# Instance normalisation bound by DMA: engine programs without a block, a first store that waits for half of the fourth load, and a last tile in three pieces

## The chip, the cores and the metric

One core of one Trainium2 chip. The metric is device time in microseconds (us) of one execution; lower is better. "Span" is the time from the first to the last instruction in a profiled execution. Every run quoted was classed fast unless it is said otherwise; each ratio is of kernels run in the same rounds on one chip. Where medians of different rounds, and so of different chips, are set side by side, the text says so; the kernel before had medians of 1248.44 to 1248.65 us in all of them.

## The reference

```python
x: (8, 64, 32, 64, 64) float32
mean = np.mean(x, axis=(2, 3, 4), keepdims=True)
var = np.var(x, axis=(2, 3, 4), keepdims=True)
return ((x - mean) / np.sqrt(var + eps)).astype(np.float32)
```

There are 512 instances of 131,072 elements, 268 MB in and 268 MB out, and each instance needs its own mean and variance.

## The kernel before

A tile holds 8 instances: 128 partitions of 8192 columns, 4 MB (16 partitions for an instance). Six slots in SBUF take turns. SyncE loads, VectorE and ScalarE each sum half of the columns, TensorE averages over the partitions of an instance with a small matrix, ScalarE squares, takes the root, and both engines scale half of the tile in place. ScalarE then issues the store. A load into a slot waits for the store of the tile that was there before. Of 64 tiles, 60 run in loops of six, three more are written out, and the last is cut in halves.

```python
    block = ctx.enter_context(nc.Block())

    @block.sync
    def _(eng):
        for s in range(SLOTS):
            eng.dma_start(out=slots[s][:], in_=x_t[s]).then_inc(landed[s], 16)
        ...
        with eng.Fori(1, ROUNDS) as it:
            for s in range(SLOTS):
                eng.dma_start(out=slots[s][:], in_=x_t[it * SLOTS + s])._wait_ge(
                    stored[s], c16
                ).then_inc(landed[s], 16)
    ...
    def on_scalar(eng, t, lane, n, c1, c2, c16, dst):
        # (cut: sum, squares with accumulation, square root)
        eng.activation(out=t[:, :w], in_=t[:, :w], func=Act.Identity,
            scale=a[:, 5:6], bias=a[:, 6:7],
        )._wait_ge(shifted[lane], c1).then_inc(done[lane], 1)
        eng.dma_start(out=dst, in_=t)._wait_ge(done[lane], c2).then_inc(stored[lane], 16)
```

## Time and profile before

| | before |
|---|---|
| time, median of 3 runs | 1248.36 us (1248.33 to 1248.52) |
| span of the profiled run | 1246.9 us |
| DMA | full in all slices but the first two and the last, 431 GB/s over the span |
| ScalarE busy | 986 us, 79% |

Read this kernel from its DMA: no compute engine limits it. The prediction below shows the slices and windows. From the page's DMA issues (KB of each, median us from issue to landing):

```profile
slot<-in_x_dram SPq DMA_DIRECT2D x63, 4096.0 KB, 52.8
out_dram<-slot ACTq DMA_DIRECT2D x63, 4096.0 KB, 45.3
```

A tile passes every 19.4 us, so 2.7 loads and 2.3 stores stand in their queues at any time; neither queue runs empty.

From its timeline, the issue of the first and of the last store on ScalarE (start, duration):

```profile
31.85 0.40 ACTq L130 DMA_DIRECT2D out_dram<-slot  x1
...
1233.92 0.34 ACTq L130 DMA_DIRECT2D out_dram<-slot  x1
```

And the last microseconds in the windows view, whose last two columns are DMA share and GB/s:

```profile
1242.00:1244.00 2.00, 0.00 (x0) 0.00 (x0) 0.00 (x0) 0.00 (x0) 0.00 (x0) 1.00 0.44 188
1244.00:1245.00 1.00, 0.00 (x0) 0.00 (x0) 0.00 (x0) 0.00 (x0) 0.00 (x0) 1.00 0.04 16
1245.00:1246.00 1.00, 0.00 (x0) 0.00 (x0) 0.00 (x0) 0.00 (x0) 0.00 (x0) 1.00 0.00 0
```

### The profile page before, as it was taken

How to read it: one execution, taken by the hardware profiler on the slowest of the kernel's cores; microseconds unless marked ns; L12 is line 12 of the kernel's file. 1: busy time of each engine (PE TensorE's matmuls, PEld its weight loads, DVE VectorE, ACT ScalarE, POOL GpSimd, SP SyncE). 2: the span in 40 equal slices, each digit the busy share in tenths (PEclk: the TensorE clock that was granted, in tenths of full speed). 3: DMA queues.
4: the chain of work that ended last, by engine and by line, in shares of the span. 5: the costliest groups of instructions: out<-in, count | busy, mean ns of one | idle time of the engine just before them, and what ended most of it. 6: DMA issues, size and time to landing. Idle time of an engine off the chain costs nothing.

```text
span 1246.9 us, 1819 instructions
## 1 busy us (share of the span) xinstructions
PE 76.4 (6%) x260; PEld 65.2 (5%) x260; DVE 467.9 (38%) x325; ACT 986.1 (79%) x410; POOL 1.9 (0%) x11
## 2 busy tenths in 40 slices
PE   0000000000000000000000000000000000000000
PEld 0000000000000000000000000000000000000000
DVE  2344334433334334343343433433334333343331
ACT  5888888887787878778777878787787878778774
POOL 0000000000000000000000000000000000000000
DMA  9999999999999999999999999999999999999998
GB/s 403 422 435 427 433 436 435 428 433 436 435 428 433 437 434 429 432 436 435 431 430 436 436 434 425 437 436 435 427 434 436 435 428 433 436 435 428 433 432 376
DMA packets 18723, 536.90 MB, mean 431 GB/s; under 512 B 2081, under 2 KB 2081, under 8 KB 2081
## 3 DMA queue, kind: packets, MB, share of 16 engines
q1 hardware_dynamic: 9360, 268.44, 50.0%
q10 hardware_dynamic: 9360, 268.44, 49.9%
q14 instruction: 3, 0.02, 0.0%
HBM read 268.44 MB, written 268.44 MB: 431 GB/s over the span
## 4 chain that ended last, share of the span: by engine, by line
ACT 48%; DVE 29%; another core or an unknown queue 13%; PE 6%; issue 1%; DMA 1%; ACTq 0%; DVEq 0%; SPq 0%
ACT unused L113 37%; DVE small L79 18%; DVE slot L95 8%; ACT slot L123 4%; ACT unused L107 4%; PE psum L136 3%; PE psum L143 3%; ACT small L120 1%; ACT L120 1%; DMA slot<-in_x_dram 1%; DVE small L89 1%; DVE small L82 1%; DVE small L92 1%; ACTq L130 0%
## 5 line engine op out<-in xcount | busy, mean ns | idle before, releaser
L113 ACT ACTIVATE unused<-slot,small 128x8192 uint8<-128x8192 f32 (+1 forms) x65 | 456.1, 7017 | 90.1 <-DVE small L82 90.1
L79 DVE TENSOR_REDUCE small<-slot 128x1 f32<-128x4096 f32 (+1 forms) x65 | 282.9, 4353 | 164.4 <-DMA slot<-in_x_dram 164.4
L107 ACT ACTIVATE unused<-slot 128x4096 uint8<-128x4096 f32 (+1 forms) x65 | 231.7, 3564 | 82.1 <-DMA slot<-in_x_dram 77.0
L123 ACT ACTIVATE slot<-slot,small 128x4096 f32<-128x4096 f32 (+1 forms) x65 | 243.7, 3749 | 27.6 <-DVE small L92 27.6
L89 DVE RECIPROCAL small<-small 128x1 f32<-128x1 f32 x65 | 10.6, 164 | 533.8 <-ACT small L120 533.8
L95 DVE TENSOR_SCALAR slot<-slot,small 128x4096 f32<-128x4096 f32 (+1 forms) x65 | 154.7, 2379 | 2.4
L136 PE MATMUL psum<-small,avg 128*128 128x2 f32 x130 | 38.2, 363 | 674.1 <-DVE small L79 548.7
L136 PEld LDWEIGHTS psum<-small,avg 128*128 128x128 f32 x130 | 32.6, 311 | 679.6 <-DVE small L79 553.0
L143 PE MATMUL psum<-small,avg 128*128 128x1 f32 x130 | 38.2, 363 | 480.6 <-ACT unused L113 480.6
L143 PEld LDWEIGHTS psum<-small,avg 128*128 128x128 f32 x130 | 32.7, 312 | 486.2 <-ACT unused L113 486.2
L120 ACT ACTIVATE small<-psum,eps_t 128x1 f32<-128x1 f32 x65 | 17.0, 261 | 37.4 <-PE psum L143 37.3
L82 DVE TENSOR_REDUCE small<-psum 128x1 f32<-128x2 f32 x65 | 10.3, 159 | 62.5 <-PE psum L136 62.5
L107 ACT ACT_TABLE_LOAD x10 | 12.8, 1283 | 10.4 <-ACT slot L123 7.1
L120 ACT ACT_TABLE_LOAD x10 | 12.8, 1283 | 0.2
L107 ACT ACTIVATION_READ_ACCUMULATOR unused<-slot 128x1 f32 x65 | 12.1, 186 | 0.0
L113 ACT ACTIVATION_READ_ACCUMULATOR unused<-slot,small 128x1 f32 x65 | 12.1, 186 | 0.0
L92 DVE TENSOR_TENSOR small<-small 128x1 f32<-128x1 f32 x65 | 10.3, 159 | 2.2
L208 POOL TENSOR_SCALAR_AFFINE_SELECT avg<-avg 128x128 f32<-128x128 f32 x4 | 1.3, 324 | 0.3
L205 POOL MEMSET avg<- 128x128 f32 x2 | 0.4, 204 | 0.5 <-SPq L42 0.5
L257 POOL MEMSET const-bfloat16-1.0<- 128x1 bf16 x1 | 0.1, 101 | 0.0
L257 POOL MEMSET const-uint8-127<- 128x1 uint8 x1 | 0.1, 101 | 0.0
L257 POOL MEMSET const-float32-0.0<- 128x1 f32 x1 | 0.1, 98 | 0.3 <-issue 0.3
(2 smaller groups left out, 0.2 us busy)
## 6 DMA issues: line engine op xcount, KB each, us to landing
slot<-in_x_dram SPq DMA_DIRECT2D x63, 4096.0 KB, 52.8
out_dram<-slot ACTq DMA_DIRECT2D x63, 4096.0 KB, 45.3
slot<-in_x_dram SPq DMA_DIRECT2D x2, 2048.0 KB, 55.6
out_dram<-slot ACTq DMA_DIRECT2D x2, 2048.0 KB, 14.7
```

Source lines behind the costliest of these rows:

```text
L79: eng.reduce_sum(out=a[:, 0:1], in_=t[:, :w], axis=mybir.AxisListType.X)._wait_ge(landed[lane], c16).then_inc(summed[lane], 1)
L82: eng.tensor_reduce(out=a[:, 2:3], in_=psum[lane][:, 0:2], axis=mybir.AxisListType.X, op=Alu.add, negate=True,)._wait_ge(meaned[lane], c1) ...
L89: eng.reciprocal(out=a[:, 5:6], in_=a[:, 4:5])._wait_ge(rooted[lane], c1).then_inc(scaled[lane], 1)
L92: eng.tensor_mul(out=a[:, 6:7], in0=a[:, 2:3], in1=a[:, 5:6])._wait_ge(scaled[lane], c1).then_inc(shifted[lane], 1)
L95: eng.tensor_scalar(out=t[:, w:], in0=t[:, w:], scalar1=a[:, 5:6], scalar2=a[:, 6:7], op0=Alu.mult, op1=Alu.add,)._wait_ge(shifted[lane], ...
L107: eng.activation(out=unused[:, w : 2 * w], in_=t[:, w:], func=Act.Identity, accum_out=a[:, 1:2],)._wait_ge(landed[lane], c16).then_inc(sum ...
L113: eng.activation(out=unused[:, : 2 * w], in_=t, func=Act.Square, bias=a[:, 2:3], accum_out=a[:, 3:4],)._wait_ge(centred[lane], c1).then_in ...
L120: eng.activation(out=a[:, 4:5], in_=psum[lane][:, 2:3], func=Act.Sqrt, bias=eps_t[:, 0:1])._wait_ge(varied[lane], c1).then_inc(rooted[lane ...
L123: eng.activation(out=t[:, :w], in_=t[:, :w], func=Act.Identity, scale=a[:, 5:6], bias=a[:, 6:7],)._wait_ge(shifted[lane], c1).then_inc(don ...
L136: eng.matmul(out=psum[lane][:, 0:2], lhsT=avg[n][:], rhs=a[:, 0:2], start=True, stop=True,)._wait_ge(summed[lane], c2).then_inc(meaned[lan ...
L143: eng.matmul(out=psum[lane][:, 2:3], lhsT=avg[n][:], rhs=a[:, 3:4], start=True, stop=True,)._wait_ge(squared[lane], c1).then_inc(varied[la ...
L208: eng.affine_select(out=m[:], in_=m[:], pattern=[[sign * split, n], [0, split]], compare_op=Alu.is_ge, fill=0.0, base=0 if sign < 0 else s ...
```

## The change

Its intent, in its author's words: looped engine programs without a block; the first store waits for the middle of the fourth load, so store and load ends alternate; last tile in three pieces (4, 2 and 2 instances). Beside these, ScalarE loads one activation table early, and the compiler then places no others, where it had placed two in each round of six tiles; and SyncE, not ScalarE, waits for the last stores. Cut to its core:

```diff
-    for h in range(2):
-        k = 2 * (n_tiles - 1) + h
-        ...
+    PIECES = [(FULL // 2, 0), (FULL // 4, FULL // 2), (FULL // 4, 3 * FULL // 4)]
+    MIDWAY = 3
     ... (in on_vector)
+        if lane == MIDWAY:
+            eng.wait_ge(midway, 16)
     ... (in on_scalar)
+        if lane == 0:
+            eng.wait_ge(midway, 16)
         eng.dma_start(out=dst, in_=t)._wait_ge(done[lane], c2).then_inc(
             stored[lane], 16
         )
-    block = ctx.enter_context(nc.Block())
-    @block.sync
-    def _(eng):
+    def load_all(eng):
         for s in range(SLOTS):
-            eng.dma_start(out=slots[s][:], in_=x_t[s]).then_inc(landed[s], 16)
+            at = 0
+            if s == MIDWAY:
+                at = COLS // 2
+                eng.dma_start(out=slots[s][:, :at], in_=x_t[s][:, :at]).then_inc(
+                    midway, 16
+                )
+            eng.dma_start(out=slots[s][:, at:], in_=x_t[s][:, at:]).then_inc(
+                landed[s], 16
+            )
     ... (the waits for the last stores move here from ScalarE)
+    load_all(nc.sync)
+    ...
+    nc.scalar.preload_act_table(Act.Sqrt)
+    nc.scalar.wait_ge(ready, set_by)
+    over_tiles(nc.scalar, on_scalar, with_target=True)
```

More of the change, by code (lines that the diff above doesn't have):

```diff
@@ L32 @@
     ROUNDS = (n_tiles - 1) // SLOTS
-    LANES = SLOTS + 2
+    PIECES = [(FULL // 2, 0), (FULL // 4, FULL // 2), (FULL // 4, 3 * FULL // 4)]
+    LANES = SLOTS + len(PIECES)
+    MIDWAY = 3
     x_f = x.rearrange("b c d h w -> (b c) (d h w)")
@@ L38, with rows @@
     out_t = out_f.rearrange("(k i) (s f) -> k (i s) f", i=FULL, s=P // FULL)
-    x_h = x_f.rearrange("(k i) (s f) -> k (i s) f", i=FULL // 2, s=2 * P // FULL)
-    out_h = out_f.rearrange("(k i) (s f) -> k (i s) f", i=FULL // 2, s=2 * P // FULL)
+    def rows(ap, first, n):
+        return ap[first : first + n].rearrange("i (s f) -> (i s) f", s=P // n)
     ctx.enter_context(tc.tile_critical(name="norm"))
@@ L50 @@
     eps_t = sbuf("eps_t", [P, 1])
-    avg = {n: sbuf(f"avg{n}", [P, P]) for n in (FULL, FULL // 2)}
+    avg = {n: sbuf(f"avg{n}", [P, P]) for n in sorted({FULL} | {n for n, _ in PIECES})}
     small = [sbuf(f"small{i}", [P, 8]) for i in range(LANES)]
-    psum = [
-        ctx.enter_context(nc.psum_tensor(f"psum{i}", [P, 512], fp32))
-        for i in range(LANES)
+    banks = [
+        ctx.enter_context(nc.psum_tensor(f"psum{i}", [P, 512], fp32)) for i in range(8)
     ]
+    psum = [banks[i % 8] for i in range(LANES)]
     def semaphores(name, n):
         return [ctx.enter_context(nc.semaphore(f"{name}{i}")) for i in range(n)]
-    ready = semaphores("ready", 1)[0]
+    ready, midway = semaphores("start", 2)
     landed = semaphores("landed", LANES)
@@ L156 @@
     last = (n_tiles - 1) % SLOTS
-    for h in range(2):
-        k = 2 * (n_tiles - 1) + h
-        half = slots[last][:, h * COLS // 2 : (h + 1) * COLS // 2]
-        rest.append((x_h[k], out_h[k], half, SLOTS + h, 1, FULL // 2))
+    for j, (n, at) in enumerate(PIECES):
+        first = (n_tiles - 1) * FULL + at
+        part = slots[last][:, at * COLS // FULL : (at + n) * COLS // FULL]
+        rest.append(
+            (rows(x_f, first, n), rows(out_f, first, n), part, SLOTS + j, 1, n)
+        )
+    MATRICES = [(m, n, 1.0 / n_elem) for n, m in avg.items()]
     def over_tiles(eng, step, with_target=False):
@@ L176, in over_tiles @@
             step(eng, t, lane, n, c, 2 * c, 16 * c, *more)
-    block = ctx.enter_context(nc.Block())
-    @block.sync
-    def _(eng):
+    def load_all(eng):
         for s in range(SLOTS):
-            eng.dma_start(out=slots[s][:], in_=x_t[s]).then_inc(landed[s], 16)
+            at = 0
[6 more added lines that the diff above has]
+                landed[s], 16
+            )
         c16 = ctx.enter_context(eng.register("load_c16"))
@@ L197, in _, with set_up @@
             )
-    @block.gpsimd
-    def _(eng):
+        for lane in range(LANES):
+            uses = sum(1 for r in rest if r[3] == lane) + (ROUNDS if lane < SLOTS else 0)
+            eng.wait_ge(stored[lane], 16 * uses)
+    def set_up(eng):
         count = 0
-        for n, m in avg.items():
+        for m, n, value in MATRICES:
             split = P // n
-            eng.memset(m[:], 1.0 / n_elem).then_inc(ready, 1)
+            eng.memset(m[:], value).then_inc(ready, 1)
             count += 1
@@ L218, in _ @@
         eng.memset(eps_t[:], eps_f).then_inc(ready, 1)
-    READY = 3 * len(avg) + 1
-    @block.vector
-    def _(eng):
-        over_tiles(eng, on_vector)
-    @block.tensor
-    def _(eng):
-        eng.wait_ge(ready, READY)
-        over_tiles(eng, on_tensor)
-    @block.scalar
-    def _(eng):
-        eng.wait_ge(ready, READY)
-        over_tiles(eng, on_scalar, with_target=True)
-        for s in range(SLOTS):
-            uses = ROUNDS + sum(1 for r in rest if r[3] == s)
-            eng.wait_ge(stored[s], 16 * uses)
-        for s in range(SLOTS, LANES):
-            eng.wait_ge(stored[s], 16)
+        return count + 1
+    load_all(nc.sync)
+    set_by = set_up(nc.gpsimd)
+    over_tiles(nc.vector, on_vector)
+    nc.tensor.wait_ge(ready, set_by)
+    over_tiles(nc.tensor, on_tensor)
+    nc.scalar.preload_act_table(Act.Sqrt)
+    nc.scalar.wait_ge(ready, set_by)
+    over_tiles(nc.scalar, on_scalar, with_target=True)
 _INS = ['x', 'eps']
```

## The prediction

> **What bounds the kernel now.** I read the slices of the whole span first, then the DMA queues, then windows cut at the two edges, then the timeline of the steady state and of the last tile.
>
> From the page of the kernel before, the DMA rows of the 40 slices and the two data queues (q1 loads, q10 stores):
>
> ```profile
> DMA  9999999999999999999999999999999999999998
> GB/s 403 422 435 427 433 436 435 428 433 436 435 428 433 437 434 429 432 436 435 431 430 436 436 434 425 437 436 435 427 434 436 435 428 433 436 435 428 433 432 376
> q1 hardware_dynamic: 9360, 268.44, 50.0%
> q10 hardware_dynamic: 9360, 268.44, 49.9%
> ```
>
> The 16 DMA engines are full in every slice except a little of the first two and the last. Nothing else is: ScalarE, the busiest engine, is at 79%. The two queues share the engines evenly.
>
> The windows view (columns: stretch and its length, busy us and count of PE, PEld, DVE, ACT, POOL, the clock, DMA share, GB/s) shows where the stream is not at its full rate:
>
> ```profile
> 0.00:2.00 2.00, 0.00 (x0) 0.00 (x0) 0.00 (x0) 0.00 (x0) 1.04 (x8) 1.00 0.00 0
> 2.00:34.00 32.00, 1.18 (x4) 1.01 (x4) 10.88 (x6) 19.26 (x9) 0.84 (x5) 1.00 1.01 426
> 34.00:40.00 6.00, 0.59 (x2) 0.50 (x2) 0.92 (x2) 5.13 (x3) 0.00 (x0) 1.00 1.04 388
> 40.00:620.00 580.00, 36.41 (x124) 31.11 (x124) 225.80 (x155) 476.37 (x197) 0.00 (x0) 1.00 1.00 433
> 620.00:1200.00 580.00, 35.25 (x120) 30.11 (x120) 219.41 (x150) 458.15 (x189) 0.00 (x0) 1.00 1.00 433
> 1200.00:1234.00 34.00, 2.94 (x10) 2.51 (x10) 10.87 (x13) 27.18 (x16) 0.00 (x0) 1.00 1.00 431
> 1234.00:1242.00 8.00, 0.00 (x0) 0.00 (x0) 0.00 (x0) 0.00 (x0) 0.00 (x0) 1.00 1.01 434
> 1242.00:1245.00 3.00, 0.00 (x0) 0.00 (x0) 0.00 (x0) 0.00 (x0) 0.00 (x0) 1.00 0.31 131
> 1245.00:1246.90 1.90, 0.00 (x0) 0.00 (x0) 0.00 (x0) 0.00 (x0) 0.00 (x0) 1.00 0.00 0
> ```
>
> The reader is to see that from 40 to 1242 us the rate is 431 to 434 GB/s. It is a floor: in the packet records nearly all 32 KB packets take 1213 ns, one begins on each engine every 1209.6 ns, and 16 engines at 32,768 B per 1.2096 us are 433.4 GB/s. The 536.87 MB (64 tiles of 4 MB, in and out) thus need 1238.6 us. What is left of the 1246.9 us span, from the same packet records:
> - 2.06 us before the first data packet (the first load is issued at 1.03);
> - 0.75 us because each engine's first packet takes some 1.9 us and not 1.21;
> - 0.87 us at 34 to 40 us, where the stores begin: the load packets in flight then take up to 2.0 us;
> - 0.8 us of slow drift, 0.01 us a tile, the 9 ns packets that increment semaphores;
> - at the end the first engine finishes at 1242.90 and the last at 1244.89, 1.8 us behind the mean engine, then 2.0 us to the end of the span: 0.48 until ScalarE has seen the last store, 0.39 for the exit of the block with its barrier, 1.05 for the closing barriers.
>
> Sum: 1238.6 + 2.06 + 0.75 + 0.87 + 0.8 + 1.8 + 2.0 = 1246.9. The time is 1.46 us above the span (1248.36). So everything that this change can touch is under 9 us, 0.7% of the time, and most of that it does not touch.
>
> **What the Trainium skill says.** "DMA: Bandwidth & Descriptors", section "Queues, rings and completion order": each DMA engine takes turns between the queues that have work, packet by packet. The trace agrees and sharpens it. A packet here is one row of a partition: 32 KB for a whole tile, 16 KB for a half tile. With equal rows loads and stores get half each; against 32 KB stores the 16 KB rows of the last two halves should get a third. The timeline shows it by the start of each tile's sum on VectorE:
>
> ```profile
> 1174.91 4.42 DVE L79 TENSOR_REDUCE small<-slot 128x1 f32<-128x4096 f32 x1 [3.13 <-DMA slot<-in_x_dram]
> ...
> 1194.30 4.42 DVE L79 TENSOR_REDUCE small<-slot 128x1 f32<-128x4096 f32 x1 [3.10 <-DMA slot<-in_x_dram]
> ...
> 1223.48 2.29 DVE L79 TENSOR_REDUCE small<-slot 128x1 f32<-128x2048 f32 x1 [1.71 <-DMA slot<-in_x_dram]
> ```
>
> A tile lands 19.4 us after the one before it, twice 4.19 MB / 433.4 GB/s = 9.68. The two halves took 29.2 us, three times 9.68.
> The same page, section "Where 436 GB/s comes from", puts the ceiling of 16 engines at 435.2 GB/s; the 433 here agrees, so the middle has no slack.
> "ScalarE: Activation LUTs", section "What ACT_TABLE_LOAD costs": 1283 ns a load; the page of this kernel has 20 loads at 1283.
> "Advanced Engine Details and Errata", section "Control Flow Timing": some 51 ns for an unconditional branch. Not shown separately here; SyncE has 0.13 us between its start branch and the first load issue.
>
> **The change part by part.**
>
> *No block.* Each engine loses a branch into its program; the exit barrier goes, and SyncE instead of ScalarE waits for the stores and goes straight to the closing steps. Start: about 0.05 us. End: 0.39 us lie between ScalarE's last wait and the step that closes the program; a branch stays on SyncE, so I count 0.25. Both lie on the path: **-0.3 us**.
>
> *Table loads.* The new program has one load, early, instead of one per function per round. That takes 1.28 us out of 19.4 us of a tile that ScalarE spends partly idle, and 1.28 out of the first tile's chain, which then waits for the half load anyway. Nothing on the path: **0**.
>
> *Third matrix on GpSimd.* The first took 0.95 us, so the set-up ends near 4 us instead of 3; it is needed when the first tile lands (13.5). **0**.
>
> *The first store waits for half of the fourth load.* Before, it is issued at 31.85 (ready by computation) and its first packet runs at 35.95, 4.1 us later, behind load packets already in flight. Now: the third load lands at 31.7 to 32.5, half a tile alone takes 4.84, so the half lands at 36.6 to 37.4; plus 0.3 for the wait the store is issued near 37.7. With the same lead its packets begin at 41 to 42. Meanwhile the loads run alone, at the same 433 GB/s, and six have been queued since 4 us, 6 x 9.68 = 58 us of work. So the queue never runs dry: **0** for the delay itself. The stores come 6 us later and the loads 6 us earlier for the whole run. Load seven is issued when the first store ends, 60 to 62, while loads five and six still occupy their queue to about 80: no gap. The second store is issued some 17.4 us after the first (ScalarE's spacing while it catches up), near 55, before the first ends: no gap there either. As to the stated aim, I doubt it: before, load four ended at 48.4 to 50.0, store one at 54.4 to 56.1, load five at 67.9, so the ends already alternated, 6 and 13 us apart. With a lead of 4 us the new store begins just as load four ends, so they would end nearly together. With both queues full I see no price or gain in either.
>
> *Smaller rows.* A 16 KB packet takes 611 ns, against half of 1213 = 606.5: 9 ns fixed a packet, as 1213 = a + f and 611 = a/2 + f give f = 9. Extra packets on each engine: 8 for the fourth load in two, and for the last tile 24 instead of 16 in each direction, so 8 + 8 + 8 = 24 packets x 9 ns, and a few semaphores: **+0.25 us**.
>
> *Three pieces at the end.* Loads end 6 us earlier in phase, so the last tile's loads begin near 1185. Its 16 KB half at a third: 14.5 us, to 1199.5 (+2.5 for the slowest engine). Its 8 KB quarters at a fifth of the engines: 1 MB is 2.42 us alone, 12.1 us each, to 1223.7, landed about 1226. That is no earlier than the 1223.5 of before. The chain of a half took 10.44 us from landing to issue (1223.48 to 1233.92). A quarter saves 1.06 of the sum, 1.7 of the squares, 0.85 of the scaling, by the halving steps seen between 8192 and 4096 columns: 6.8 us. Last store issued near 1233. What DMA still has to do then: the remaining stores, full until the last quarter is due at about 1240.4. So the last store is in the queue 7 us before its turn, where it was 4 us before. But before there was no gap (434 GB/s from 1234 to 1242), so the margin buys nothing: **0**.
>
> Sum: -0.3 + 0.25 = about 0. Two terms of the edges may shrink by accident or design, the 0.87 us of the store start (half-size packets are then in flight) and the 1.8 us of the slowest engine at the end; I take 0.4 off for them. Predicted 1247.9 us.
>
> **Rivals.**
> (a) *Coinciding ends cost, alternating ends gain.* If simultaneous ends leave an engine a bubble, and my reckoning that they now coincide is right, 60 tiles at 0.03 us would be +2 us: 1250. If instead they alternate better, the gain is bounded by the 0.8 us drift plus part of the end spread: 1247. Against both: no slice or window of the middle is below full rate.
> (b) *A gap in the tail.* If the quarters' loads are slower than a fifth, or the stores run ahead, the stream runs out before the last quarter is stored. Each us of lateness beyond the 7 us margin costs one: up to 1250. For it: small rows against large ones do starve. Against: ScalarE's chain and the backlog as worked out.
> (c) *The start of the stores gets cheaper* because it falls on a boundary of loads with small packets: at most -0.87: 1247.0.
>
> **Range and chances.** The three runs of before lie within 0.2 us, so noise is small beside the terms. The likely corrections are -0.9 to +1: 1246.7 to 1249.0. Faster by 2% would need 25 us, three times all that is not pure transfer: 0.5%. Slower by 2% would need the stream to dry up repeatedly: 0.5%.
>
> **What would show each step right or wrong.** Right: 433 GB/s in both long windows; ScalarE with one table load; first store issue near 37.7; the last loads landing near 1226; no dip before the final 2 us; about 1.7 us from the last packet to the end. Wrong: a window in the middle below 431 or above 434, a hole between 1200 and 1242, a first store packet well before 40, or a first load issue earlier than 0.9 us.

## More of the kernel before

One of sixteen engines is a share of 0.0625. After 1244 us about one engine still works, and it is done before 1245.

## The result

| | before | changed |
|---|---|---|
| first comparison, median | 1248.44 us (4 runs, 1248.33 to 1250.5) | 1249.62 us (4 runs, 1248.98 to 1250.92) |
| five more rounds (experiment e1), median | 1248.53 us (11 runs, 1248.32 to 1248.67) | 1249.53 us (5 runs, 1248.94 to 1250.3) |

The ratio of the first comparison is 1.0007 (95% interval 0.999 to 1.0024), that of the five rounds 1.001 (0.9997 to 1.0023). These ratios are not quite those of the medians. The changed kernel's median is about 1 us later in both sets, and it scatters over 1.4 to 1.9 us. The kernel before is calmer but not free of it: of its 37 runs in all rounds of this document, 4 took 1250.5 to 1250.8 us and the others at most 1248.80. The prediction, 1247.9 us and at most 1249.0, was too low.

The slices of the changed kernel's page still show a full stream:

```profile
DMA  9999999999999999999999999999999999999998
GB/s 403 419 433 429 434 431 434 435 432 434 429 434 436 431 434 431 433 435 432 433 432 431 435 434 432 431 433 434 435 430 433 432 434 434 432 435 429 433 434 347
```

Only the last slice is clearly lower, 347 against 376 GB/s. Next the page's groups and DMA issues:

```profile
L247 ACT ACT_TABLE_LOAD x1 | 1.3, 1283 | 1.0 <-SPq L48 1.0
...
out_dram<-slot ACTq DMA_DIRECT2D x63, 4096.0 KB, 59.9
slot<-in_x_dram SPq DMA_DIRECT2D x62, 4096.0 KB, 38.5
```

One table load is left. Stores now stand 14.6 us longer in their queue and loads 14.3 us shorter, but the rate is unchanged, as two windows of the middle show:

```profile
46.00:620.00 574.00, 36.40 (x124) 31.10 (x124) 225.43 (x155) 467.21 (x187) 0.00 (x0) 1.00 1.00 433
620.00:1200.00 580.00, 35.22 (x120) 30.09 (x120) 219.41 (x150) 448.69 (x181) 0.00 (x0) 1.00 1.00 433
```

The timeline has the first store's issue, the start of the last quarter's sum (its load has landed) and the last store's issue:

```profile
37.71 0.40 ACTq L140 DMA_DIRECT2D out_dram<-slot  x1
...
1228.49 1.22 DVE L87 TENSOR_REDUCE small<-slot 128x1 f32<-128x1024 f32 x1 [3.90 <-DMA slot<-in_x_dram]
...
1235.31 0.34 ACTq L140 DMA_DIRECT2D out_dram<-slot  x1
```

The difference is in the end of the windows view:

```profile
1242.00:1244.00 2.00, 0.00 (x0) 0.00 (x0) 0.00 (x0) 0.00 (x0) 0.00 (x0) 1.00 0.63 266
1244.00:1245.00 1.00, 0.00 (x0) 0.00 (x0) 0.00 (x0) 0.00 (x0) 0.00 (x0) 1.00 0.12 49
1245.00:1246.00 1.00, 0.00 (x0) 0.00 (x0) 0.00 (x0) 0.00 (x0) 0.00 (x0) 1.00 0.08 33
1246.00:1247.00 1.00, 0.00 (x0) 0.00 (x0) 0.00 (x0) 0.00 (x0) 0.00 (x0) 1.00 0.08 33
1247.00:1248.00 1.00, 0.00 (x0) 0.00 (x0) 0.00 (x0) 0.00 (x0) 0.00 (x0) 1.00 0.02 8
```

A share of 0.08 and then 0.02 is about one engine: from 1245.4 us on a single DMA engine works alone. The packet records give its end exactly. Before, the first engine completes the last store at 1242.90, the fifteenth at 1244.02, the last at 1244.89. Changed, these are 1242.89, 1245.34 and 1247.56. So the last engine ends 2.67 us later. The distance from there to the time of that same run shrank from 3.71 us (1248.6 - 1244.89) to 3.36 (1250.92 - 1247.56), and 2.67 - 0.35 = 2.32 us is the whole difference of the two profiled runs. The profiled run of the changed kernel is its slowest; e1 below has one of its fastest.

Where that engine lost its time stands in the packet records too. A 32 KB packet normally takes 1213 ns. In this run 20 store packets between 51 and 114 us took 38 to 387 ns more, together 3.45 us. But for two longer pauses they follow each other at steps of 2.5 to 2.8 us. That is the step of one engine that serves its two queues by turns (twice 1.21 us and the delay), so they are put down to one engine; the records do not name it. The ends of the first four stores spread over the engines by 4.2, 5.9, 6.7 and 7.1 us (1.7 us before); then the spread stays at 7.1 to the end of the loop. In the kernel before no store packet is more than 25 ns late between 50 and 1200 us.

### The profile page after: what moved, and what is told of

It is laid out like the page before. It is cut to its first block, busy times and chain, and to the rows that moved or that the text cites. A ratio compares the mean times of both kernels' runs of the same rounds, so it can differ in the third digit from the quotient of the medians. Undisturbed runs are those within 1.5% of the kernel's fastest.

```text
span 1249.2 us, 1825 instructions
## 1 busy us (share of the span) xinstructions
PE 77.5 (6%) x264; PEld 66.2 (5%) x264; DVE 468.3 (37%) x330; ACT 963.0 (77%) x397; POOL 2.6 (0%) x14
## 3 DMA queue, kind: packets, MB, share of 16 engines
q1 hardware_dynamic: 9648, 268.44, 49.9%
## 4 chain that ended last, share of the span: by engine, by line
another core or an unknown queue 70%; ACT 14%; DMA 10%; SPq 2%; PE 1%; DVE 1%; issue 1%; ACTq 0%
ACT unused L121 7%; DMA slot<-in_x_dram 6%; DMA out_dram<-slot 4%; ACT slot L131 4%; ACT unused L115 3%; SPq L206 1%; PE psum L153 1%; PE psum L146 1%; DVE small L87 0%; ACTq L140 0%; ACT small L128 0%; DVE small L97 0%; DVE small L90 0%; DVE small L100 0%
```

## The experiments

The first question is whether this is the midway wait, the pieces or chance; the second what it is about the wait. All ran in five rounds beside the kernel before. The second column of the table has the moment at which the first store is issued and that at which its first packet runs. The times of all runs:

| experiment | first store issued, data (us) | runs, us | before in the same rounds: median (range) |
|---|---|---|---|
| e1 repeat | 37.68, 41.91 | 1248.94 1248.99 1249.53 1250.29 1250.30 | 1248.53 (1248.32 to 1248.67) |
| e2 no midway | 31.00, 35.00 | 1248.31 1256.57 1256.68 1257.62 1257.87, and 1279.77 (slow) | as e1 |
| e3 halves | 37.86, 42.28 | 1248.42 1248.71 1248.82 1249.85 1250.29 | as e1 |
| e4 midway alone | 37.86, 42.41 | 1248.99 1249.04 1249.11 1249.35 1249.56 | as e1 |
| e5 quarter | 35.51, 39.44 | 1249.49 1249.60 1249.78 1249.94 1257.16 1257.39 | 1248.65 (1248.40 to 1250.78) |
| e6 three quarters | 40.23, 44.48 | 1280.90 1283.66 1287.81 1288.16 1288.88 | as e5 |
| e7 whole fourth load | 42.48, 46.94 | 1248.97 1249.17 1249.18 1250.35 1250.42 | as e5 |
| e8 tables back, no wait | 31.69, 36.17 | 1248.29 1248.41 1248.44 1248.55 1248.66 | as e5 |
| e9 third load | 33.06, 37.36 | 1249.75 1249.78 1249.80 1249.83 1249.95 | 1248.50 (1248.35 to 1248.74) |
| e10 no midway, halves | 31.12, 36.18 | 1248.36 1248.42 1254.36 1254.98 1257.07 1258.89 | as e9 |
| e11 tables back, halves | 31.63, 36.28 | 1248.19 1248.30 1248.33 1248.49 1248.64 | as e9 |
| e12 third load, halves | 33.19, 37.34 | 1248.91 1249.48 1249.53 1249.65 1249.86 | as e9 |
| e13 filler | 31.96, 36.05 | 1248.71 1249.72 1250.19 1250.38 1250.47 | 1248.54 (1248.36 to 1250.76) |
| e14 tables, third load | 32.94, 37.39 | 1249.63 1249.65 1249.67 1249.70 1249.77 | as e13 |
| e15 no midway again | 31.17, 36.04 | 1248.20 1256.61 1256.77 1259.56 1261.36 1266.77 | as e13 |

The second column is from each experiment's profiled run, which is one of the runs listed. In e10 and e15 it was a run of the lower mode (1248.36 and 1248.20).

### e1 to e4: which part

**e1** is the changed kernel, unaltered.

> The changed kernel again, unaltered, to learn how far its times scatter. Theory A (delaying the first store makes one DMA engine's stores run slow for some 60 us near the start): median 1249 to 1250.5, scatter of 1 to 2 us, while the kernel before stays within 0.3 us; in the profile one engine ends 3 to 5 us after the first. Theory B (the 8 KB rows of the last quarters cost it): median 1249 to 1250, but scatter as small as before's. Theory C (it is chance, in either kernel): both scatter alike by 1 to 2 us and their medians agree within 0.5.

Median 1249.53, over a range of 1.36 us; the kernel before stayed within 0.35 us in the same rounds. So in these rounds the scatter belongs to the changed kernel (theory A, not C). In this profiled run (1248.99) the slow store packets near the start were all but absent: 0.04 us in all between 46 and 130 us; its last engine ends 2.38 us after the first, not 3 to 5. The slow stretch of the first profile is thus an event of some runs, not the whole cause.

**e2** takes the midway wait and the split away and keeps everything else.

```diff
-    MIDWAY = 3
+    MIDWAY = None
-        if lane == 0:
-            eng.wait_ge(midway, 16)
```

> The changed kernel without the midway wait and without the split of the fourth load; no block and three pieces are kept. Theory A: 1248.0 to 1248.4, scatter 0.3, no store packets above 1213 ns after the first 15 us of storing, last engine 2 us behind the first at the end. Theory B: as the changed kernel, 1249.5. Theory C: scatter as wide as the changed kernel's.

No theory had this: one run at 1248.31, four between 1256.6 and 1257.9, and one at 1279.77. Without its wait the changed program is worse, not better. The windows of a 1257.62 us run:

```profile
620.00:1200.00 580.00, 35.23 (x120) 30.09 (x120) 216.33 (x150) 445.08 (x180) 0.00 (x0) 1.00 1.00 433
1234.00:1242.00 8.00, 1.17 (x4) 1.00 (x4) 1.29 (x4) 4.26 (x6) 0.00 (x0) 1.00 0.75 316
1242.00:1248.00 6.00, 0.65 (x3) 0.56 (x3) 1.38 (x2) 3.24 (x4) 0.00 (x0) 1.00 0.36 147
1248.00:1256.00 8.00, 0.53 (x2) 0.44 (x2) 1.14 (x3) 1.50 (x2) 0.00 (x0) 1.00 0.37 154
```

The stream runs dry from 1234 us on, which is rival (b) of the prediction. Its timeline says why:

```profile
1243.70 1.06 ACT L115 ACTIVATE unused<-slot 128x1024 uint8<-128x1024 f32 x1 [3.48 <-DMA slot<-in_x_dram]
...
1250.52 0.34 ACTq L138 DMA_DIRECT2D out_dram<-slot  x1
```

The last quarter is ready for its sum only at 1243.70 and its store is issued at 1250.52. On the first engine the last quarter's load had ended at 1223.4, on the last at 1243.3. All through the run single engines lose 0.03 to 0.5 us on a few packets of each tile (20.6 us of engine time between 130 and 1150 us), so that the ends of one load spread over the engines by 1.7 us at the fourth load and by 12.6 us at the sixty-third. The mean stream hardly notices: it is still 433 GB/s. But a tile is summed only when its slowest engine has landed.

**e3** gives the changed kernel its two halves back.

```diff
-    PIECES = [(FULL // 2, 0), (FULL // 4, FULL // 2), (FULL // 4, 3 * FULL // 4)]
+    PIECES = [(FULL // 2, 0), (FULL // 2, FULL // 2)]
```

> The changed kernel with its last tile in two halves again, as before; midway wait and no block are kept. Theory A: 1249 to 1250.5 with wide scatter, as the changed kernel. Theory B: 1248.1 to 1248.3. Theory C: wide scatter in all, including the kernel before.

Means 1249.22 against e1's 1249.61 (medians 1248.82 and 1249.53), ranges that overlap almost wholly: the pieces are not shown to cost anything, and the scatter remains. Theory B (the 8 KB rows) falls.

**e4** adds the midway wait and the split load, in the code of the diff above, to the kernel before, and nothing else.

> The kernel before with the midway wait and the split fourth load alone (block, table loads and two halves kept). Theory A: 1249.3 to 1251, wide scatter: the changed kernel's time plus the 0.23 us of the block's exit. Theory B: 1248.4, narrow. Theory C: wide scatter in all.

Median 1249.11, against 1248.53 before; theory A had at least 1249.3 and a wider scatter. All five runs lie above all eleven of before. So the wait, with the split load that it needs, brings a loss of 0.6 us at the medians while the block and the table loads stay in place. By the ratio alone, 1.0005 (0.9992 to 1.0017), it would not be clear of noise; the separation of the runs is what shows it. In its profile the last engine ends 1.78 us after the fifteenth (0.87 us in the kernel before), and its time is again 3.72 us after that end, as before, where the versions without a block have 3.34 to 3.51. The end of its windows:

```profile
1244.00:1245.00 1.00, 0.00 (x0) 0.00 (x0) 0.00 (x0) 0.00 (x0) 0.00 (x0) 1.00 0.08 33
1245.00:1246.00 1.00, 0.00 (x0) 0.00 (x0) 0.00 (x0) 0.00 (x0) 0.00 (x0) 1.00 0.04 16
```

### e5 to e8: what about the wait

These vary what the first store waits for. In e5 and e6 the edit is `at = COLS // 4` and `at = 3 * COLS // 4` in place of `COLS // 2`. e7 is:

```diff
-    MIDWAY = 3
+    MIDWAY = None
         if lane == 0:
-            eng.wait_ge(midway, 16)
+            eng.wait_ge(landed[3], 16)
```

e8 is e2 without the line `nc.scalar.preload_act_table(Act.Sqrt)`.

> The changed kernel with the first store waiting for a quarter of the fourth load. Theory F (an engine slips by some 0.1 to 0.4 us a tile while its load ends and its store ends lie within about 3 us of each other, and not otherwise): the first store is issued near 34.5 and its data begins near 38.3, so a store ends about 12 us after one load and 7 before the next; no slips, 1248.0 to 1248.4, scatter under 0.4. Theory G (the earlier the first store, the later the last loads, and only that counts): worse than the changed kernel, 1250 to 1255. Theory H (what matters is that the per-round table loads are gone): as the changed kernel, 1249 to 1250.

> As before, but waiting for three quarters of the fourth load. Theory F: issue near 39.7, data near 43.5, load five ends near 60, store one near 62.5: a gap of about 3 us, so engines slip all the way; 1250 to 1257, or a scatter over 1.5 us, and load ends that spread over the engines by more than 4 us at the end. Theory G: no worse than the changed kernel, 1248.0 to 1249. Theory H: 1249 to 1250.

> The first store waits for the whole fourth load, which is not split. Theory F: issue near 42.4, data near 46.3, load five ends near 56, store one near 66: gaps of about 10 us on both sides; 1248.0 to 1248.5, scatter under 0.4. Theory G: 1248.0 too. Theory H: 1249 to 1250.

> The kernel without the midway wait once more (e2), but with the table loads left to every round as in the kernel before, so that the first store is issued about 1 us later, near 31.8. Theory F: the gap of load end and store end grows from 4 to 5 or 6 us, as in the kernel before: 1248.1 to 1248.5, scatter under 0.5, no hole in the last 30 us. Theory G: barely better than e2: 1254 to 1257. Theory H: 1248.1 as well.

e6 is the largest effect, 1287.81 us at the median, +39 us for a wait that differs by a quarter of one load; its ratio to before is 1.0291 (1.027 to 1.0312). Its page shows the whole stream slowed and a ragged end:

```profile
GB/s 401 423 419 424 426 427 434 425 421 429 427 425 431 424 426 428 428 422 421 427 421 426 427 427 428 426 427 429 424 428 427 425 427 432 422 426 421 420 355 191
```

In it the first load after the start of the stores ends at 59.5 to 60.6 us and the first store at 62.8 to 64.6, so some 3 us apart as reckoned, and the late packets of the next tiles come in bursts just as a store ends. Theory F had the direction and far too small a size. e8 held to it too: 1248.44, no scatter. But e5, with load ends and store ends 11 and 9 us apart, should have been calm and had two of six runs at 1257 us, and e7, with 8 and 11 us, should have been at 1248.5 at most and was at 1249.18. So the distance of the ends does not decide it alone. Theory G falls with e6. Theory H asks that the table loads be tested by themselves. e8's last windows:

```profile
1242.00:1244.00 2.00, 0.00 (x0) 0.00 (x0) 0.00 (x0) 0.00 (x0) 0.00 (x0) 1.00 0.73 299
1244.00:1245.00 1.00, 0.00 (x0) 0.00 (x0) 0.00 (x0) 0.00 (x0) 0.00 (x0) 1.00 0.06 25
1245.00:1246.00 1.00, 0.00 (x0) 0.00 (x0) 0.00 (x0) 0.00 (x0) 0.00 (x0) 1.00 0.00 0
```

One engine works alone for about 1 us, as in the kernel before.

### e9 to e12: the moment of the first store, and a version that might beat both

e9 is e7 with `landed[2]`, e10 is e2 with two halves, e11 is e8 with two halves, and e12 is e9 with two halves.

> The changed kernel with the first store waiting for the whole third load, so with one table load as in e2, but with the first store issued near 32.6 and its data near 36.9, within 1 us of the kernel before. Theory F' (only the offset of store ends after load ends counts: 5.4 to 6 us is calm, 3 to 4 us is bad, whatever sets it): offset near 7, 1248.2 to 1248.7, scatter under 0.5, under 1 us of extra packet time. Theory H (the missing table loads themselves do the harm): as e2, 1254 to 1280.

> e2 with the last tile in two halves. Theory F' with a tail part (the engines slip as in e2, some 9 to 12 us between the first and the last at the end of the loads, and the 8 KB rows make the last engine later still): the same spread of load ends as e2, but 1250 to 1254 and not 1257. If the pieces have no part in it: 1257 again.

> e8 with two halves: the kernel before without its block and nothing else of the change. Theory F': 1248.1 to 1248.3, 0.25 below before (the block's exit), scatter under 0.4. If small rows cost nothing: equal to e8 in its rounds, else 0.15 below it.

> e9 with two halves. Theory F': 1248.1 to 1248.5, like e11, and the candidate for a version better than both kernels. Theory H: as e10.

e9 came out at 1249.80 within 0.2 us, so neither calm at 1248.5 nor in the bad mode: a miss for both theories. Its first store is issued only 1.2 us later than that of the kernel before. e10 has the two modes of e2 (two runs near 1248.4, four between 1254 and 1259), so halves do not cure it; whether quarters make the bad mode worse is not separated. e11, the kernel before without its block, is at 1248.33 against 1248.50, ratio 0.9999 (0.9986 to 1.0012). e12 is at 1249.53, again a miss for both theories. Nothing beats the kernel before by more than its scatter; e8 and e11 equal it.

### e13 to e15: the table loads or the moment

e13 puts two small ScalarE operations ahead of the first store of each round, into scratch tiles of their own, so that the single table load stays and the first store comes at about the old moment. e14 is e9 without the early table load. e15 repeats e2 on the same chip.

```diff
+        if lane == 0:
+            eng.activation(out=sink[0][:], in_=avg[FULL][:], func=Act.Identity)._wait_ge(
+                done[lane], c2
+            ).then_inc(fill_a, 1)
+            eng.activation(out=sink[1][:], in_=avg[FULL][:], func=Act.Identity)._wait_ge(
+                fill_a, c1
+            ).then_inc(fill_b, 1)
+            eng.wait_ge(fill_b, c1)
         eng.dma_start(out=dst, in_=t)._wait_ge(done[lane], c2)
```

> e2 (one table load, no midway wait, three pieces) with two small ScalarE operations ahead of the first store of each round, which delay it by some 0.7 us, to about 31.7. If only the moment of the first store counts: 1248.2 to 1248.7 in all runs, like e8. If the missing table loads do harm of their own: as e2, some runs at 1254 to 1280.

> e8 (table loads as before, three pieces) with the first store waiting for the whole third load, issued near 33.1 as in e9. If only the moment counts: 1249.5 to 1250 in all runs, like e9, its last engine over 3 us behind the first. If the single table load was the harm in e9: 1248.3 to 1248.6.

> e2 unaltered, on the chip of e13 and e14. Both theories: two modes again, some runs near 1248.3 and some at 1254 to 1280. If all runs are near 1248.3, the modes belong to a chip or a day and e13 proves nothing.

e15 shows the two modes on this chip too: one run at 1248.20, five at 1256.6 to 1266.8. e13 has no run in the bad mode, with the same single table load: 1248.71 to 1250.47. So a missing table load by itself is not what makes the bad mode. What ended it here is the filler, which issues the first store 0.8 us later and also delays one store in each later round; e13 does not separate the two. But e13 did not reach e8's calm either, although its first store is issued only 0.27 us later than e8's, and its first packet runs 0.12 us earlier: a miss for both theories. e14 has all its table loads and is at 1249.67, like e9, as the moment alone had it: there too the moment of the first store matters, and the tables do not help. At the last store its last engine ends 2.79 us behind the first, a little under the 3 expected. Its last windows show the lone engine that e8 does not have after 1245 us:

```profile
1244.00:1245.00 1.00, 0.00 (x0) 0.00 (x0) 0.00 (x0) 0.00 (x0) 0.00 (x0) 1.00 0.06 25
1245.00:1246.00 1.00, 0.00 (x0) 0.00 (x0) 0.00 (x0) 0.00 (x0) 0.00 (x0) 1.00 0.08 33
1246.00:1247.00 1.00, 0.00 (x0) 0.00 (x0) 0.00 (x0) 0.00 (x0) 0.00 (x0) 1.00 0.00 0
```

### What the packet records say across the runs

For eleven of the seventeen profiled runs: when the last store ends on the fifteenth and on the last engine, the distance from there to that run's time, and the sum of all lateness of 32 KB packets over 1213 ns between 130 and 1150 us. Left out are e3, e10 and e12, which lie in the same ranges (the last engine at 1244.87 to 1245.44), and the profiled runs in the bad mode, e2, e5 and e6, with 20.6, 53.3 and 256.5 us of late packets.

| run | time | 15th engine | last engine | time minus last | late packets, us |
|---|---|---|---|---|---|
| before | 1248.60 | 1244.02 | 1244.89 | 3.71 | 1.66 |
| e15 | 1248.20 | 1243.53 | 1244.73 | 3.47 | 1.65 |
| e11 | 1248.33 | 1243.67 | 1244.85 | 3.48 | 1.60 |
| e8 | 1248.55 | 1243.74 | 1245.08 | 3.47 | 1.84 |
| e1 (changed) | 1248.99 | 1244.26 | 1245.48 | 3.51 | 1.81 |
| e4 | 1249.56 | 1244.06 | 1245.84 | 3.72 | 1.69 |
| e14 | 1249.77 | 1243.86 | 1246.31 | 3.46 | 2.79 |
| e9 | 1249.83 | 1243.98 | 1246.37 | 3.46 | 2.54 |
| e13 | 1250.19 | 1244.29 | 1246.74 | 3.45 | 3.14 |
| e7 | 1250.35 | 1244.43 | 1246.86 | 3.49 | 3.34 |
| changed, first | 1250.92 | 1245.34 | 1247.56 | 3.36 | 2.02 |

Three readings. First, the time is the last engine's end plus a constant, 3.7 us with the block and 3.4 to 3.5 without. Second, the fifteenth engine ends within 1.0 us in all but one run, while the last one moves by 2.8 us. Third, in e7, e9, e13 and e14 the extra 0.9 to 1.7 us of late packets falls on that one engine: in e13, for example, a store's ends spread by 2.06 us near 150 us and by 4.73 near 1145, but without the last engine still by 2.06. Some three to five packets of each tile take 5 to 33 ns more. In e4 and in e1 the sum of late packets is as small as in the kernel before; there the engines were already further apart near 120 us, where the ends of a store spread by 2.3 and 3.5 us (1.7 before).

One thing in every trace looks like a cause of the lone engine and is not shown to be one. Two instruction fetches, 8 KB packets of 309 ns, stand among the data, and a data packet that starts where one of them ends is late. In e11 they come at 105 us (the next packet 248 ns late) and at 1192 us (351 ns), 1.22 us in all. But e11's last engine is 1.08 us behind the fifteenth near 1160 us and 1.07 near 1212: its lag grew by some 0.03 us a tile long before the second fetch and took no step at it.

## Why the prediction was wrong

**Bound.** Right for the rate: the middle runs at 433 GB/s in both kernels, and no part of the change moved that. Three of the small terms around it do not come out of the records as stated: the first packets cost 0.62 us on the mean engine, not 0.75; the last engine is 1.58 us behind the mean one, not 1.8; and the time of the profiled run is 1.7 us above its span (1248.60, 1246.89), as the 1.46 set the median of other runs against it. None of them bears on the forecast change.

**No block.** Right in sum: the end shortened by 3.71 - 3.45 = 0.26 us (before and e4 against most versions without a block, in which SyncE also waits for the last stores), predicted 0.25 at the end. The start gave 0.006 us (first load issued at 1.029, then at 1.023 by the trace), predicted 0.05.

**Table loads.** The group shows one left, as said. A load cost 1.28 us and no more: in the kernel before one stands from 26.04 to 27.32 us, and the next operation starts at 27.34. "Nothing on the path" held only because the midway wait hides it: without that wait the first store comes 0.7 us earlier than with the tables, and e2 and e15 fall into a mode of 1254 us and more. The prediction did not look at the single table load without the wait.

**Third matrix.** Right: set up by 3.87 us, needed at 13.24.

**First store.** Every time in this step was right: issued at 37.71 (predicted near 37.7), first data at 41.63 (41 to 42), load five ends at 62.8 to 64.2 and store one at 59.2 to 63.4, so nearly together, and the queues never ran dry. The conclusion was the step that failed: "With both queues full I see no price or gain in either." e4 isolates it at +0.6 us; in the program without a block it comes to about 1.1 (e1 against e8, in different rounds, where the table loads differ too). The step reasoned about the sum of sixteen engines, which indeed kept its rate in the middle, and took from it that the end could not move. The end is set by one engine. Rival (a) came nearest, with 1250 us, but reckoned with a bubble on every engine at every end; measured is a last engine that ends 0.6 us (e1) to 2.7 us (first profile) later.

**Allowance for edges.** "I take 0.4 off" was wrong in sign. The turnaround where the stores begin cost 0.87 us before, and 0.8 and 1.1 us in the two profiles of the changed kernel, so nothing was saved there, and the lateness of the slowest engine grew: 2.67 us in the first profile, 0.59 in that of e1 (1245.48 - 1244.89).

**Smaller rows.** Predicted +0.25 us; not seen. e1 against e3 lies within their scatter, and e8 and e11, from different rounds, differ by 0.11 us. The working took 9 ns a packet from durations that overlap. By their starts on the engine that ends alone, 16 KB packets follow each other every 607 ns (before) and 8 KB packets every 306 ns (changed), so some 5 ns a packet are fixed and 24 packets come to an estimated 0.12 us.

**Three pieces.** The last quarter's sum began at 1228.49 (predicted landing 1226), its chain took 6.82 us (predicted 6.8), and the last store was issued 5.1 us before the quarter ahead of it began to end at 1240.4, against the 7 us reckoned. No gap appeared, as predicted. e2 shows that rival (b) is real when the engines drift apart.

**What stays open.** That a wait before the first store alone changes the time of the whole run is shown where nothing else in the program differs: by e12 against e10 in the same rounds, and in different rounds by e14 against e8 (+1.2 us) and e9 and e7 against e2 and e15. e6 against the changed kernel (+38 us) differs also in how the fourth load is cut (24 and 8 KB rows, not 16 and 16). e13 is weaker evidence, as its filler also delays one store in each later round. Why the moment matters so is not shown. Bursts of late packets at store ends in e6 suggest that the ends of the two queues' transfers disturb each other on an engine when they come some 3 us apart, but e5 and e7 contradict a rule by distance alone, and no run here separates the semaphore writes at the ends, the fetch of new descriptors and the addresses in flight. The profiled bad run of e2 differs from the good ones of e10 and e15 in one visible point: two of the sixteen engines began the first store 1.2 us, one packet, before the rest, where in e10 and e15 all sixteen began within 0.5 us. But in the kernel before four engines began 1.6 to 2.0 us after the first, and it is calm; so this is a place to look, not a cause. The author's aim, that ends alternate, could not be confirmed as a benefit: they already alternated before, and they coincide after. But in the program with one table load the wait does help: 1249.5 us where e2 and e15 have 1257 to 1258.

## What to carry to other kernels

Where DMA is full from end to end, as here, the time is set by the slowest of the sixteen engines, so after such a change read the last few microseconds first: a share near 0.06 is one engine alone. Moving the first store by one to three microseconds changed the time by anything between nothing and 38 us here, by a mechanism that stays open, so time such a change in several rounds and look for modes, not only at a median. And judge the parts together: the wait that costs 0.6 us in one program saves some 8 in another.

## What the Trainium skill lacked or had wrong

- "DMA: Bandwidth & Descriptors", "Queues, rings and completion order", describes the turns between queues, and the runs agree: two full queues get 50.0 and 49.9% of the engines. Nothing there or elsewhere says that the moment at which the second queue starts can change the time for the whole run: 1248.4 us at 31.7 us, two modes at 1248.3 and 1254 to 1267 at 31.0 to 31.2, 1249.8 at 33, 1287.8 at 40.2. The moment is not the whole rule: e13 had 1248.7 to 1250.5 us at 32.0.
- The same page, "Latency and other measured facts", calls engines 7 and 15 usually slower and gives a guess for transfers issued by GpSimd. Here all data transfers are issued by SyncE and ScalarE, and still one engine ends last, 0.9 to 2.5 us after the fifteenth in the table above (the records do not say which number it has).
- "Runtime: NRT & Kernel Launch", "Instruction fetch mechanics", says that an engine's sequencer fetches its next instructions through a DMA queue of its own and that the cost is mostly hidden. It does not say that the fetch takes a turn among the data packets: in every trace here two fetch packets of 309 ns stand among them, each with a data packet 0.11 to 0.54 us late behind it. What that costs the whole time is not shown.
- "DMA: Bandwidth & Descriptors", "Where 436 GB/s comes from", says that for transfers between HBM and SBUF the HBM side at about 358 GB/s binds. Here it does not: these runs, with one core of the chip at work, hold 433 GB/s, half reads and half writes, close to the 435 GB/s that the section gives for the port side.
- "Advanced Engine Details and Errata", "Control Flow Timing", gives some 51 ns for a branch. No run here measures a branch by itself; without the block the first load is issued 6 ns earlier (1.029 and 1.023 us).
